# A quad's first difference behind the split before it, and buffers of their own for odd units' residual rows

## The chip, the cores and the metric

The program runs on one core of one Trainium2 chip. The metric is device time in microseconds (us) of one execution. The engines: PE (TensorE) multiplies matrices, DVE (VectorE) and ACT (ScalarE) do elementwise work, POOL (GpSimd) and SP (SyncE) here mostly issue transfers (DMAs). Each engine works its own queue of instructions in order.

## The reference

Two layers over 256 rows of 2048 values in float32, each with a norm, a wide input projection, attention over 32 heads of 128, a gate, and an output projection that is added to the residual:

```python
def reference(x, a_norm, a_w_in, a_rel_bias, a_w_out, kv_norm, kv_w, f_w, f_b,
              b_norm, b_w_in, b_w_out, final_norm):
    for layer in range(DEPTH):
        if layer < N_A_LAYERS:
            h = rms_norm(x, a_norm[layer])
            q, k, v, g = jnp.split(h @ a_w_in[layer], 4, axis=-1)
            o = chunked_relbias_attention(split_heads(q), split_heads(k), split_heads(v),
                                          a_rel_bias[layer]).reshape(b, s, D_INNER)
            x = x + (o * jax.nn.silu(g)) @ a_w_out[layer]
        else:
            ...
            h = rms_norm(x, b_norm[lb])
            q, g = jnp.split(h @ b_w_in[lb], 2, axis=-1)
            o = forgetting_attention(split_heads(q), k_sh, v_sh, cum_logf_h).reshape(b, s, D_INNER)
            x = x + (o * jax.nn.silu(g)) @ b_w_out[lb]
    return rms_norm(x, final_norm)
```

Keys, values and forget gates of layer B (`k_sh`, `v_sh`, `cum_logf_h`) are products of a norm of the same rows. The change touches the two output projections, the addition of the residual behind them, and the start of layer B.

## The kernel before

Matrix products are made exact to float32 by splitting: each weight block is loaded raw (`ao_raw`, 512 KB), ACT rounds it to a high part (`ao_hi`, L247), DVE takes the rest (`ao_lo`, L248), and PE makes three products of high and low parts (L184). The same happens in layer B with a gain factor (`bqg_hi` L242, `bqg_lo` L243). `Feed` loads blocks on SP in one given order, six raw buffers deep, and splits them three blocks ahead of PE.

The output projection of layer A runs from about 700 to 877 us, that of layer B from 1586 to 1754. Each has four units (u = 0 to 3) of 512 output columns and 16 blocks each. Unit u's sums of 256 rows stand in two PSUM tiles, `ao_acc` or `bo_acc`.

Part of the blocks are multiplied for two units at once, by a scheme that saves products (class `Quad`): the same block of two units, `one` and `two` (loaded one after the other, `two` later), is turned into four operands by differences on DVE. The first, A (L287), is `two − one`; the second, B (L288), takes one half of `two` from the other; later ones (L296, L297) write into `one`. Each operand is split (`quad_hi` L293 on ACT, `quad_lo` L294 on DVE). In layer A the pair of units 0 and 1 has three quads and the pair 2 and 3 has five, in layer B the pair 2 and 3 has five. Between two quads stand three plain blocks. The quads' partial products `p` are joined when the pair's last quad is done (L336 to L340, into `ao_quad`, read as `quads.comb`), and have to be added to each unit's rows.

Closing a unit (`ao_closed`): DVE adds the joined quads to the residual rows `xin` (L751, 128x1024) and then the two PSUM tiles (L753). `xin` was loaded by SP when the unit had four blocks left (L743, 512 KB, from `in_x`; in layer B from `x1d`). All `xin` share one buffer (tag "R"), so a load waits until the unit before has let go of it. SP stores the new rows to `x1d`. Then the rows are turned for layer B: for units 0 to 2 by a DVE transpose into `xinY` (L486) and 16 small POOL transfers into `xinZ` (L489, 32 KB each), which ACT and DVE split into `x1Th` and `x1Tl` (L150, L151). `xinY` is one buffer, so the next unit's transpose waits until all 16 transfers of the unit before have landed. Unit 3 is turned by PE (`xT`, L169), inside the first unit of layer B, `bqg0`, behind its second block (`{1: 99}` in the drive at L877). `bqg0` reads the turned rows in order, units 0 and 1 in its first four blocks, unit 2 from its fifth, unit 3 from its seventh.

At the end, `bo_closed` adds quads and sums likewise (L924, L889), squares the rows on ACT for the final norm (L890), and `finish_tile` scales and stores them.

The order of instructions on each engine is not that of the code: a scheduler places each instruction where its operands are expected, so an instruction that takes part in a dependency may be placed elsewhere. `feed.behind(dst, n)` (L261 to L264) is used for that: a tiny ACT copy of two columns of a block's high part into `dst`. Whatever then writes `dst` on another engine must follow that split.

Of the kernel before, what the change touches and what calls it, by code (L numbers as in the profile page):

```python
# [9 lines left out]
F32 = mybir.dt.float32  # L10
# [6 lines left out]
P = 128  # L17
S = 256
NT = S // P
# [16 lines left out]
UN = 512  # L36
# [23 lines left out]
B1_STEPS = {3: 1, 5: 1, 6: 2}  # L60
B2_STEPS = {1: 1}
OLD_B_STEPS = {0: 1, 1: 99}
# [3 lines left out]
def r32(ap):  # L66
    return ap.bitcast(F32)
# [8 lines left out]
def trunk(ctx, tc, x, x_t, gains, a_w_in, a_rel, a_w_out, kv_w, f_w, f_b, b_w_in, b_w_out, final_norm, out):  # L76
    nc = tc.nc
    pe, act, dve, pool, sp = nc.tensor, nc.scalar, nc.vector, nc.gpsimd, nc.sync
# [4 lines left out]
    att = ctx.enter_context(tc.tile_pool(name="att", bufs=1))  # L83
# [8 lines left out]
    def big_tile(shape, dt, name):  # L92
        return big.tile(shape, dt, name=name, tag="big")
# [46 lines left out]
    def advance(side, n=1):  # L140
        if side is not None:
            for _ in range(n):
                next(side, None)
# [18 lines left out]
    def x_to_T(src, k0):  # L162

        banks = []
        for c in range(0, 4, 2):
            ps = bank(f"xT_{k0 + c}")
            for i in range(2):
                for t in range(NT):
                    pe.transpose(ps[:, i * S + t * P:i * S + (t + 1) * P],  # L169
                                 src[t][:, (c + i) * P:(c + i + 1) * P], ident)  # L170
            banks.append(ps)
        for c in range(4):
            split_x1(banks[c // 2][:, c % 2 * S:(c % 2 + 1) * S], k0 + c)
            yield
# [102 lines left out]
    class Quad:  # L277
# [4 lines left out]
        def split(self, i):  # L282

            one, two = self.raw
            t = self.all.t[:, 0]
            if not i:
                dve.tensor_sub(t[:, :, 0], two[:, :, 0], one[:, :, 0])  # L287
                dve.tensor_sub(t[:, :, 1], two[:, :, 1], two[:, :, 0])  # L288
            src = [one, t, two[:, :, 1:], one][i]
            n = src.shape[2]  # L290
            hi = stream.tile([P, IL, KB, HN], F32R, name=f"quad_hi{i}", tag="hi", bufs=SPLIT)
            lo = stream.tile([P, IL, KB, HN], F32R, name=f"quad_lo{i}", tag="lo", bufs=SPLIT)
            act.activation(hi[:, :, :n], src, AF.Copy)  # L293
            dve.tensor_sub(lo[:, :, :n], src, r32(hi[:, :, :n]))  # L294
            if not i:
                dve.tensor_sub(one[:, :, 0], two[:, :, 1], t[:, :, 0])  # L296
                dve.tensor_sub(one[:, :, 1], one[:, :, 1], one[:, :, 0])  # L297
            return hi, lo
# [100 lines left out]
    ao_quads, bo_quads = Quads("ao", a_w_out), Quads("bo", b_w_out)  # L399
# [12 lines left out]
    feed = Feed(todo)  # L412
# [26 lines left out]
    def unit(lhs):  # L439
        yield from rest(Unit(lhs, next(order)))  # L440

    def rest(u):

        for b in range(u.nk // KB - u.left, u.nk // KB):
            u.step(b)
            yield u.acc
# [218 lines left out]
    def side_a(g, accs):  # L665
        tb = att.tile([P, HG, S], F32, name="tb", tag="tb")
        for lo_, hi_, c0 in ((0, CHUNK, CHUNK), (CHUNK, P, 0)):
            sp.dma_start(out=tb[lo_:hi_, :, c0:], in_=bass.AP(
                tensor=a_rel.tensor, offset=a_rel.offset + g * HG * NREL + REL + 1 - P + lo_ + c0,
                ap=[[1, hi_ - lo_], [NREL, HG], [1, S - c0]]))  # L670

        def biases():
            pool.memset(tb[:CHUNK, :, :CHUNK], NEG)
            return tb[:, :, ::-1], tb[:, :, P - 1::-1]

        qk = rows(UN, "qk")
        evac_scaled(accs["qk"], 0, UN, rsA, qk)
        yield

        def vg():  # L680
            return accs["v"], accs["g"]

        yield from attention(g, biases, qk, vg, halfA, oA, (pool, pool, pool, act), (2, 2), home)
# [5 lines left out]
    def drive(gen, side, steps, hooks={}, old=None, old_steps={}):  # L689

        acc = None
        for i, acc in enumerate(gen):
            advance(old, old_steps.get(i, 0))
            advance(side, steps.get(i, 0))
            if i in hooks:
                hooks[i]()
        return acc
# [12 lines left out]
    rs, prev = [], None  # L710
    for g in range(NG):
        accs = {}
# [7 lines left out]
        old, prev = prev, side_a(g, accs)  # L720
# [5 lines left out]
    x1T = Stat("x1T", KD)  # L726

    def x1_to_T(xin, u):
        z = turn(xin.rearrange("p t (c d) -> p (t c) d", d=P), NT * 4, "xin")
        xinT = z.rearrange("p i (t c) u -> p c t i u", t=NT)  # L730
        yield
        for i in range(4):
            feed.behind(x1T.h(u * 4 + i)[:, ::P][:, :, None], 2)
            for t in range(NT):
                split_x1(xinT[:, i, t], u * 4 + i,
                         lambda v: v[:, t * P:(t + 1) * P].rearrange("p (i u) -> p i u", u=SQ))
            yield

    xins, last = {}, []

    def load_xin(src, u):
        xins[u] = att.tile([P, NT, UN], F32, name="xin", tag="R")
        sp.dma_start(out=xins[u], in_=src[:, :, u * UN:(u + 1) * UN])  # L743

    def ao_begun(u, left):
        if left == 4:
            load_xin(xf, u)

    def ao_closed(u, acc):
        cs, xin = slice(u * UN, (u + 1) * UN), xins.pop(u)  # L750
        dve.tensor_add(xin, xin, ao_quads.comb[:, u % 2 * NT:u % 2 * NT + NT])  # L751
        for t in range(NT):
            dve.tensor_add(xin[:, t], acc[t], xin[:, t])  # L753
            sp.dma_start(out=x1d[:, t, cs], in_=xin[:, t])
        more = None
        if u < 3:
            more = x1_to_T(xin, u)
            next(more)
        else:
            last.append(x_to_T([xin[:, t] for t in range(NT)], u * 4))  # L760
        for t in range(NT):
            act.activation(att.tile([P, UN], F32, name="junk", tag="tb"), xin[:, t], AF.Square,
                           accum_out=ssq1[:, t, u:u + 1])
        return more and (more, [8, 1, 1, 1])
# [108 lines left out]
    old = prev = None  # L873
    fg = forget()
    for g in range(NG):
        accs = {}
        accs["qg"] = drive(unit(x1T), prev if g else last[0], B1_STEPS if g else {1: 99}, {}, old, OLD_B_STEPS)  # L877
        accs["kv"] = drive(unit(x1T), prev if g else fg, B2_STEPS if g else FORGET_STEPS, {2: lambda: open_b(accs)})
        old, prev = prev, side_b(g, accs)
        advance(prev)  # L880
# [36 lines left out]
    def bo_begun(u, left):  # L917
        if left == (4 if u else 1):
            load_xin(x1d, u)

    def bo_closed(u, acc):
        xin = xins.pop(u)
        if u > 1:
            dve.tensor_add(xin, xin, bo_quads.comb[:, u % 2 * NT:u % 2 * NT + NT])  # L924
        for t in range(NT):
            residual(acc, xin, u, t)
            if u == 2 and t == 1:
                norm_head()
            if u == 3:
                finish_tile(t)  # L930
# [48 lines left out]
```

## Time and profile before

| what | us |
|---|---|
| time, median of 3 runs | 1765.71 (1765.02 to 1766.46) |
| the profiled execution | 1764.38 |
| its span, first to last instruction | 1762.7 |
| PE busy | 1741.2 |
| DVE busy | 1244.9 |
| ACT busy | 1108.3 |
| POOL busy | 516.8 |

A row of the timeline reads: start, duration, engine, line, operation, what it writes and reads, count; in brackets how long the engine stood idle before and what ended that. SPq, ACTq and POOLq are the issue of transfers. A piece of the chain reads: start, duration, what. A window's row gives each engine's busy time in the stretch, the granted PE clock (1.00 is full), the transfer engines' busy share, and GB/s.

Outside the stretches that the prediction shows, PE stands still only at the start and in the B layer's attention, near 1545 us.

### The profile page before, as it was taken

To read this page: it belongs to the slowest core of one execution; us is meant where nothing else is said; L and a number is where in the kernel's file an instruction comes from. 1 tells how busy PE (TensorE), PEld (TensorE's weight loads), DVE (VectorE), ACT (ScalarE), POOL (GpSimd) and SP (SyncE) were. 2 spreads that over 40 slices of the span, in tenths; PEclk is the share of its full clock that TensorE was granted. 3 is DMA by queue.
4 is the path that set the end of the run, shared out by engine and by line. 5 is a ranking of instruction groups with operands and counts; after the bars stand their busy time and mean duration, and the time that the engine had idled before them with its cause. 6 is when DMAs were issued, how large, how long until landed. Compare 5 with 4: busy or idle time off the path is not lost.

```text
span 1762.7 us, 25633 instructions
## 1 busy us (share of the span) xinstructions
PE 1741.2 (99%) x8348; PEld 1531.0 (87%) x8348; DVE 1244.9 (71%) x1818; ACT 1108.3 (63%) x2102; POOL 516.8 (29%) x1071
## 2 busy tenths in 40 slices
PE   9999999999999999999999999999999999999997
PEld 7888888888888888887888888888888888888886
DVE  7666666666666686688877777777777777876687
ACT  6555555555555566556557777777777777765454
POOL 2333333333333333112104333333333333333000
PEclk9999999999999999999999999999999999999999
DMA  8777776767777677576767777776777777777664
GB/s 297 243 223 222 224 224 224 224 224 227 226 225 225 223 224 224 195 256 213 243 212 230 228 227 226 228 225 223 226 225 225 227 228 226 226 230 233 205 215 144
DMA packets 143653, 396.35 MB, mean 225 GB/s; under 512 B 31104, under 2 KB 38560, under 8 KB 143392
## 3 DMA queue, kind: packets, MB, share of 16 engines
q1 hardware_dynamic: 107472, 354.25, 63.1%
q0 software_dynamic: 32256, 37.29, 6.5%
q10 hardware_dynamic: 3792, 3.17, 0.6%
q8 instruction: 66, 1.08, 0.3%
q14 instruction: 67, 0.55, 0.1%
HBM read 351.05 MB, written 4.23 MB: 202 GB/s over the span
## 4 chain that ended last, share of the span: by engine, by line
PE 93%; DVE 3%; DMA 2%; issue 1%; ACT 1%; POOL 0%; ACTq 0%; SPq 0%; DVEq 0%; POOLq 0%
PE aqk_acc L184 19%; PE bkv_acc L184 19%; PE avg_acc L184 19%; PE bqg_acc L184 18%; PE bo_acc L184 6%; PE ao_acc L184 5%; PE op L574 1%; PE s0p L540 1%; DVE quad_lo L294 0%; DMA xinZ<-xinY 0%; PE op L517 0%; PE s1p L517 0%; PE s1p L516 0%; PE s1p L518 0%; PE op L518 0%
## 5 line engine op out<-in xcount | busy, mean ns | idle before, releaser
L489 POOL DMA_DIRECT2D sgZ<-sgY x512 | 251.0, 497 | 194.3 <-DVE sgY L486 90.6
L489 POOL DMA_DIRECT2D turned<-turned x448 | 219.9, 498 | 259.6 <-PE avg_acc L184 95.3
L243 DVE SCALAR_TENSOR_TENSOR bqg_lo<-bqg_raw,gain,bqg_hi 128x512 fp32r<-128x512 f32 x256 | 183.2, 753 | 84.3 <-ACT bqg_hi L242 84.2
L242 ACT ACTIVATE bqg_hi<-bqg_raw,gain 128x512 fp32r<-128x512 f32 x256 | 170.4, 714 | 106.7 <-PE bqg_acc L184 51.3
L248 DVE TENSOR_TENSOR avg_lo<-avg_raw,avg_hi 128x1024 fp32r<-128x1024 f32 x127 | 153.4, 1219 | 109.2 <-ACT avg_hi L247 108.0
L248 DVE TENSOR_TENSOR aqk_lo<-aqk_raw,aqk_hi 128x1024 fp32r<-128x1024 f32 x125 | 152.5, 1220 | 86.7 <-ACT aqk_hi L247 85.3
L247 ACT ACTIVATE avg_hi<-avg_raw 128x1024 fp32r<-128x1024 f32 x127 | 132.4, 1055 | 121.0 <-PE aqk_acc L184 68.5
L243 DVE SCALAR_TENSOR_TENSOR bkv_lo<-bkv_raw,gain,bkv_hi 128x512 fp32r<-128x512 f32 x256 | 181.2, 749 | 38.5 <-ACT bkv_hi L242 35.8
L184 PE MATMUL aqk_acc<-aqk_hi,xTh 128*128 128x512 f32 x512 | 191.4, 384 | 1.2 <-ACT aqk_hi L247 1.2
L184 PE MATMUL bqg_acc<-bqg_hi,x1Th 128*128 128x512 f32 x512 | 191.6, 384 | 0.0
L184 PE MATMUL avg_acc<-avg_hi,xTh 128*128 128x512 f32 x512 | 190.3, 382 | 0.0
L184 PE MATMUL aqk_acc<-aqk_lo,xTh 128*128 128x512 f32 x512 | 189.6, 381 | 0.0
L184 PE MATMUL aqk_acc<-aqk_hi,xTl 128*128 128x512 f32 x512 | 189.6, 381 | 0.0
L184 PE MATMUL bkv_acc<-bkv_hi,x1Th 128*128 128x512 f32 x512 | 189.2, 380 | 0.0
L184 PE MATMUL bqg_acc<-bqg_lo,x1Th 128*128 128x512 f32 x512 | 189.0, 379 | 0.0
L184 PE MATMUL bqg_acc<-bqg_hi,x1Tl 128*128 128x512 f32 x512 | 189.0, 379 | 0.0
L184 PE MATMUL bkv_acc<-bkv_lo,x1Th 128*128 128x512 f32 x512 | 189.0, 379 | 0.0
L184 PE MATMUL avg_acc<-avg_lo,xTh 128*128 128x512 f32 x512 | 189.0, 379 | 0.0
L184 PE MATMUL bkv_acc<-bkv_hi,x1Tl 128*128 128x512 f32 x512 | 189.0, 379 | 0.0
L184 PE MATMUL avg_acc<-avg_hi,xTl 128*128 128x512 f32 x512 | 189.0, 379 | 0.0
L247 ACT ACTIVATE aqk_hi<-aqk_raw 128x1024 fp32r<-128x1024 f32 x125 | 131.6, 1053 | 91.1 <-PE aqk_acc L184 43.5
L242 ACT ACTIVATE bkv_hi<-bkv_raw,gain 128x512 fp32r<-128x512 f32 x256 | 168.7, 712 | 22.9 <-PE bqg_acc L184 16.7
(297 smaller groups left out, 3563.8 us busy)
## 6 DMA issues: line engine op xcount, KB each, us to landing
bqg_raw<-in_b_w_in SPq DMA_DIRECT2D x128, 512.0 KB, 4.3
bkv_raw<-in_kv_w SPq DMA_DIRECT2D x128, 512.0 KB, 4.0
avg_raw<-in_a_w_in SPq DMA_DIRECT2D x127, 512.0 KB, 4.3
aqk_raw<-in_a_w_in SPq DMA_DIRECT2D x125, 512.0 KB, 4.2
ao_raw<-in_a_w_out SPq DMA_DIRECT2D x64, 512.0 KB, 4.4
bo_raw<-in_b_w_out SPq DMA_DIRECT2D x64, 512.0 KB, 4.2
sgZ<-sgY POOLq DMA_DIRECT2D x512, 40.0 KB, 4.1
turned<-turned POOLq DMA_DIRECT2D x448, 32.0 KB, 3.7
```

The source lines that it names most:

```text
L184: pe.matmul(acc[t], x[:, t * P:(t + 1) * P], w, start=t not in begun, stop=last and i == 2)
L242: act.activation(hi[:, :, j], raw[:, :, j], AF.Copy, scale=gk)
L243: dve.scalar_tensor_tensor(lo[:, :, j], raw[:, :, j], gk, r32(hi[:, :, j]), op0=OP.mult, op1=OP.subtract)
L247: act.activation(hi[:, :, j], raw[:, :, j], AF.Copy)
L248: dve.tensor_sub(lo[:, :, j], raw[:, :, j], r32(hi[:, :, j]))
L489: queues[j].dma_start(out=r32(z)[j * SQ:(j + 1) * SQ, i], in_=y[i * SQ:(i + 1) * SQ, j])
L540: pe.matmul(s0p[:, i], q0[:, i], qkT[:, HG + i, 0], start=True, stop=True)
L574: pe.matmul(op[:, i, P:], v1[:, i * DH:(i + 1) * DH], pT[:, i, NT], start=False, stop=i == HG - 1)
```

## The change

There are four edits. In `Quad.split` a copy by `feed.behind` is put ahead of the first difference, which ties A to the split of the block that precedes the quad. Rows `xin` of odd units get a tile of their own. The addition of the joined quads moves out of the closing: for odd units it comes when two blocks of the unit are left (in `add_combined`, L747 in the changed kernel). And unit 3's turn by PE goes behind the third block of `bqg0`. Lines behind L287 are one higher in the changed kernel, those behind L744 seven or more.

```diff
@@ -284,6 +284,7 @@
             one, two = self.raw
             t = self.all.t[:, 0]
             if not i:
+                feed.behind(t[:, :, 0, :1], -1)
                 dve.tensor_sub(t[:, :, 0], two[:, :, 0], one[:, :, 0])
                 dve.tensor_sub(t[:, :, 1], two[:, :, 1], two[:, :, 0])
             src = [one, t, two[:, :, 1:], one][i]
@@ -739,16 +740,22 @@
     xins, last = {}, []
 
     def load_xin(src, u):
-        xins[u] = att.tile([P, NT, UN], F32, name="xin", tag="R")
+        xins[u] = big_tile([P, NT, UN], F32, f"xin{u}") if u % 2 else att.tile([P, NT, UN], F32, name="xin", tag="R")
         sp.dma_start(out=xins[u], in_=src[:, :, u * UN:(u + 1) * UN])
+
+    def add_combined(quads, u):
+        dve.tensor_add(xins[u], xins[u], quads.comb[:, u % 2 * NT:u % 2 * NT + NT])
 
     def ao_begun(u, left):
         if left == 4:
             load_xin(xf, u)
+        if left == 2 and u % 2:
+            add_combined(ao_quads, u)
 
     def ao_closed(u, acc):
+        if u % 2 == 0:
+            add_combined(ao_quads, u)
         cs, xin = slice(u * UN, (u + 1) * UN), xins.pop(u)
-        dve.tensor_add(xin, xin, ao_quads.comb[:, u % 2 * NT:u % 2 * NT + NT])
         for t in range(NT):
             dve.tensor_add(xin[:, t], acc[t], xin[:, t])
             sp.dma_start(out=x1d[:, t, cs], in_=xin[:, t])
@@ -874,7 +881,7 @@
     fg = forget()
     for g in range(NG):
         accs = {}
-        accs["qg"] = drive(unit(x1T), prev if g else last[0], B1_STEPS if g else {1: 99}, {}, old, OLD_B_STEPS)
+        accs["qg"] = drive(unit(x1T), prev if g else last[0], B1_STEPS if g else {2: 99}, {}, old, OLD_B_STEPS)
         accs["kv"] = drive(unit(x1T), prev if g else fg, B2_STEPS if g else FORGET_STEPS, {2: lambda: open_b(accs)})
         old, prev = prev, side_b(g, accs)
         advance(prev)
@@ -917,11 +924,13 @@
     def bo_begun(u, left):
         if left == (4 if u else 1):
             load_xin(x1d, u)
+        if left == 2 and u == 3:
+            add_combined(bo_quads, u)
 
     def bo_closed(u, acc):
+        if u == 2:
+            add_combined(bo_quads, u)
         xin = xins.pop(u)
-        if u > 1:
-            dve.tensor_add(xin, xin, bo_quads.comb[:, u % 2 * NT:u % 2 * NT + NT])
         for t in range(NT):
             residual(acc, xin, u, t)
             if u == 2 and t == 1:
```

How the order of instructions moves, at three places. Names carry the unit (`ao2`, `ao3`), the block and a number of the tile.

First, DVE at the second quad of the pair of units 2 and 3 (near 805 to 814 us). Before:

```order
L294 TENSOR_TENSOR quad_lo3_7645<-ao2_raw0_7428,quad_hi3_7644 128x1024
L287 TENSOR_TENSOR ao_quad_6864<-ao3_raw1_7552,ao2_raw1_7550 128x2x256
L248 TENSOR_TENSOR ao2_lo9_7657<-ao2_raw9_7466,ao2_hi9_7656 128x1024
L248 TENSOR_TENSOR ao2_lo10_7669<-ao2_raw10_7484,ao2_hi10_7668 128x1024
L248 TENSOR_TENSOR ao2_lo11_7678<-ao2_raw11_7502,ao2_hi11_7677 128x1024
L288 TENSOR_TENSOR ao_quad_6864<-ao3_raw1_7552 128x2x256
L294 TENSOR_TENSOR quad_lo0_7694<-ao2_raw1_7550,quad_hi0_7693 128x1024
```

After:

```order
L295 TENSOR_TENSOR quad_lo3_7649<-ao2_raw0_7431,quad_hi3_7648 128x1024
L289 TENSOR_TENSOR ao_quad_6864<-ao3_raw1_7555 128x2x256
L248 TENSOR_TENSOR ao2_lo9_7661<-ao2_raw9_7469,ao2_hi9_7660 128x1024
L248 TENSOR_TENSOR ao2_lo10_7673<-ao2_raw10_7488,ao2_hi10_7672 128x1024
L248 TENSOR_TENSOR ao2_lo11_7682<-ao2_raw11_7506,ao2_hi11_7681 128x1024
L288 TENSOR_TENSOR ao_quad_6864<-ao3_raw1_7555,ao2_raw1_7553 128x2x256
L295 TENSOR_TENSOR quad_lo0_7699<-ao2_raw1_7553,quad_hi0_7698 128x1024
```

A (L287 before, L288 after) goes behind the three plain splits `ao2_lo9` to `ao2_lo11`; B (L288 before, L289 after) goes ahead of them, to the row where A stood. Both read `ao3_raw1`, the later load.

Second, SP and DVE where unit 1 closes (near 788 to 800 us). SP before, from the last load ahead of unit 1's rows to the second quad's blocks:

```order
L206 DMA ao2_raw9_7466<-in_a_w_out 128x1024
L743 DMA xin_7444<-in_x 128x2x512
L206 DMA ao2_raw10_7484<-in_a_w_out 128x1024
L206 DMA ao2_raw11_7502<-in_a_w_out 128x1024
L754 DMA x1d_6776<-xin_7444 128x512 x2
L206 DMA ao2_raw1_7550<-in_a_w_out 128x1024
L743 DMA xin_7862<-in_x 128x2x512
```

After:

```order
L206 DMA ao2_raw9_7469<-in_a_w_out 128x1024
L744 DMA xin_7868<-in_x 128x2x512
L206 DMA ao2_raw10_7488<-in_a_w_out 128x1024
L206 DMA ao2_raw11_7506<-in_a_w_out 128x1024
L761 DMA x1d_6776<-xin1_7447 128x512 x2
L206 DMA ao2_raw1_7553<-in_a_w_out 128x1024
L744 DMA xin3_8184<-in_x 128x2x512
L206 DMA ao3_raw1_7555<-in_a_w_out 128x1024
```

Unit 1's rows (`xin_7444` before, `xin1_7447` after) are loaded 36 rows ahead of their old place, unit 2's rows (`xin_7862`, `xin_7868`) stand where unit 1's stood, and unit 3's (`xin3_8184`) where unit 2's stood. DVE there before:

```order
L287 TENSOR_TENSOR ao_quad_6864<-ao3_raw0_7430,ao2_raw0_7428 128x2x256
L288 TENSOR_TENSOR ao_quad_6864<-ao3_raw0_7430 128x2x256
L248 TENSOR_TENSOR ao2_lo7_7499<-ao2_raw7_7392,ao2_hi7_7498 128x1024
L751 TENSOR_TENSOR xin_7444<-xin_7444,ao_quad_6864 128x1024
L753 TENSOR_TENSOR xin_7444<-ao1_acc0_7090,xin_7444 128x512
L753 TENSOR_TENSOR xin_7444<-ao1_acc1_7091,xin_7444 128x512
L248 TENSOR_TENSOR ao2_lo8_7547<-ao2_raw8_7410,ao2_hi8_7546 128x1024
L486 STREAM_TRANSPOSE xinY_7521<-xin_7444 128x1024
```

After:

```order
L248 TENSOR_TENSOR ao2_lo5_7466<-ao2_raw5_7341,ao2_hi5_7465 128x1024
L747 TENSOR_TENSOR xin1_7447<-xin1_7447,ao_quad_6864 128x1024
L248 TENSOR_TENSOR ao2_lo6_7485<-ao2_raw6_7350,ao2_hi6_7484 128x1024
L289 TENSOR_TENSOR ao_quad_6864<-ao3_raw0_7433 128x2x256
L248 TENSOR_TENSOR ao2_lo7_7503<-ao2_raw7_7395,ao2_hi7_7502 128x1024
L760 TENSOR_TENSOR xin1_7447<-ao1_acc0_7091,xin1_7447 128x512
L760 TENSOR_TENSOR xin1_7447<-ao1_acc1_7092,xin1_7447 128x512
L248 TENSOR_TENSOR ao2_lo8_7550<-ao2_raw8_7413,ao2_hi8_7549 128x1024
L288 TENSOR_TENSOR ao_quad_6864<-ao3_raw0_7433,ao2_raw0_7431 128x2x256
L487 STREAM_TRANSPOSE xinY_7524<-xin1_7447 128x1024
```

The add of the joined quads to unit 1's rows (L751, L747) goes ahead of two plain splits, and the row behind it is no longer that of the closing.

Third, DVE at the start of layer B (near 872 to 886 us). Before:

```order
L486 STREAM_TRANSPOSE xinY_8117<-xin_7862 128x1024
L243 SCALAR_TENSOR_TENSOR bqg0_lo0_8197<-bqg0_raw0_8078,gain_83,bqg0_hi0_8196 128x2x256
L243 SCALAR_TENSOR_TENSOR bqg0_lo1_8217<-bqg0_raw1_8090,gain_83,bqg0_hi1_8216 128x2x256 x2
L243 SCALAR_TENSOR_TENSOR bqg0_lo2_8237<-bqg0_raw2_8099,gain_83,bqg0_hi2_8236 128x2x256 x2
L243 SCALAR_TENSOR_TENSOR bqg0_lo3_8314<-bqg0_raw3_8144,gain_83,bqg0_hi3_8313 128x2x256
L751 TENSOR_TENSOR xin_8176<-xin_8176,ao_quad_6864 128x1024
L243 SCALAR_TENSOR_TENSOR bqg0_lo3_8314<-bqg0_raw3_8144,gain_83,bqg0_hi3_8313 128x2x256
L753 TENSOR_TENSOR xin_8176<-ao3_acc0_7638,xin_8176 128x512
L753 TENSOR_TENSOR xin_8176<-ao3_acc1_7639,xin_8176 128x512
```

After:

```order
L487 STREAM_TRANSPOSE xinY_8125<-xin_7868 128x1024
L243 SCALAR_TENSOR_TENSOR bqg0_lo0_8205<-bqg0_raw0_8086,gain_83,bqg0_hi0_8204 128x2x256
L747 TENSOR_TENSOR xin3_8184<-xin3_8184,ao_quad_6864 128x1024
L243 SCALAR_TENSOR_TENSOR bqg0_lo1_8226<-bqg0_raw1_8098,gain_83,bqg0_hi1_8225 128x2x256 x2
L243 SCALAR_TENSOR_TENSOR bqg0_lo2_8246<-bqg0_raw2_8107,gain_83,bqg0_hi2_8245 128x2x256 x2
L760 TENSOR_TENSOR xin3_8184<-ao3_acc0_7642,xin3_8184 128x512
L760 TENSOR_TENSOR xin3_8184<-ao3_acc1_7643,xin3_8184 128x512
L243 SCALAR_TENSOR_TENSOR bqg0_lo3_8322<-bqg0_raw3_8152,gain_83,bqg0_hi3_8321 128x2x256 x2
```

The add to unit 3's rows (`xin_8176`, `xin3_8184`) goes ahead of five splits of `bqg0`, and the closing adds go ahead of both splits of its fourth block, `bqg0_lo3`. On PE the eight matmuls of `xT` go from behind `bqg0`'s second block to behind its third, with 12 matmuls of 128x512 between.

## The prediction

> **What bounds the kernel now.** I read the page first, then the list of waits of PE (the TensorE matmul queue), then the chain and the engines' rows around each place where PE stands still.
>
> ```profile
> PE 1741.2 (99%) x8348; PEld 1531.0 (87%) x8348; DVE 1244.9 (71%) x1818; ACT 1108.3 (63%) x2102; POOL 516.8 (29%) x1071
> ```
>
> PE's waits, with the sum, their count and the longest:
>
> ```profile
> PE xT L169 <- DVE xin L753: 2.9, 2, 2.7
> PE op L516 <- ACT wideh L508: 2.6, 2, 2.2
> PE ao_acc L184 <- DVE ao_lo L248: 2.2, 1, 2.2
> PE bo_acc L517 <- DVE quad_lo L294: 0.9, 1, 0.9
> PE ao_acc L517 <- DVE quad_lo L294: 0.3, 1, 0.3
> PE p L517 <- DVE quad_lo L294: 0.3, 1, 0.3
> ```
>
> PE works in 99% of the span. No instruction of PE is removed, so the change can win only where PE waits, or behind PE's last matmul. It touches the waits named xT (2.9 us), ao_acc and p (2.2 + 0.3 + 0.3) and bo_acc (0.9), and the tail. The wait named op lies in the B layer's attention, where nothing moves. So the stake is some ten microseconds of 1764.38 (the profiled execution; its span is 1762.7), about 1.3 below the median of 1765.71. I take the sum against 1764.38 and carry it to the median.
>
> **Place 1: the second pair's first quads, 786 to 816 us.** DVE's rows:
>
> ```profile
> 793.82 1.23 DVE L751 TENSOR_TENSOR xin<-xin,ao_quad 128x1024 f32<-128x1024 f32 x1 [1.05 <-DMA xin<-in_x]
> 799.28 1.25 DVE L486 STREAM_TRANSPOSE xinY<-xin 128x1024 f32<-128x1024 f32 x1 [1.71 <-DMA xinZ<-xinY]
> 809.31 0.69 DVE L287 TENSOR_TENSOR ao_quad<-ao_raw,ao_raw 128x512 f32<-128x512 f32 x1 [1.98 <-DMA ao_raw<-in_a_w_out]
> 809.92 3.49 DVE L248 TENSOR_TENSOR ao_lo<-ao_raw,ao_hi 128x1024 fp32r<-128x1024 f32 x3
> 813.32 0.69 DVE L288 TENSOR_TENSOR ao_quad<-ao_raw 128x512 f32<-128x512 f32 x1
> ```
>
> The first difference (L287) waits 1.98 us for a weight block, and three splits stand behind it, the first of which PE needs at 811.19. The change ties L287 behind those splits. But the order of the changed kernel puts the second difference into the place that it leaves, and that one reads the later loaded block alone, the very block that L287 waited for. So DVE stops at the same point for the same transfer, and one 0.69 us instruction stands ahead of the splits as before. The tie itself costs a copy on ACT (ScalarE) for each of 13 quads:
>
> ```profile
> L264 ACT ACTIVATE x1Th<-ao_hi x2: 206/208/209, 793.8 to 825.4; 128x2 fp32r<-128x2 f32 x2
> 795.87 0.64 ACT L762 ACTIVATE junk<-xin 128x512 f32<-128x512 f32 x1 [1.87 <-DVE xin L753]
> ```
>
> 13 x 0.21 = 2.7 us of ACT, each beside idle time like the 1.87 us of the second row; without that cover all 2.7 would count. The copy follows its split at once and the new A waits for it only three splits later. **Term 1: 0**, between −2.2 (the wait gone after all) and +2.7. In the bo quads the swap is the same, and PE's 0.9 us there stays.
>
> What does move at this place is SP (the queue of the large transfers) against POOL's 16 small ones, which turn unit 0:
>
> ```profile
> 788.67 0.38 SPq L743 DMA_DIRECT2D xin<-in_x  x1
> 795.87 0.93 SPq L754 DMA_DIRECT2D x1d<-xin  x2
> 797.60 0.33 SPq L206 DMA_DIRECT2D ao_raw<-in_a_w_out  x1
> 795.64 1.02 POOL L489 DMA_DIRECT2D xinZ<-xinY  x2 [0.50 <-DMA xinZ<-xinY]
> 790.10 5.26 DMA xinZ<-xinY
> 796.17 2.99 DMA xinZ<-xinY
> 786.00:798.00 12.00, 12.00 (x57) 10.51 (x57) 8.94 (x10) 5.64 (x10) 7.87 (x16) 1.00 0.98 331
> ```
>
> Unit 1's residual rows are now loaded some 90 us before, in a buffer of their own, and the add (L751) no longer waits 1.05 us and no longer stands between the splits and unit 1's closing: two adds of 0.69 us instead of 1.23 + 2 x 0.69 behind a wait. So unit 1 closes about 2.4 us earlier (1.05 of the wait, 1.23 of the add, less little), and its two stores of 256 KB and the next 512 KB weight load are issued near 793.4, 794.1 and 795.2 in place of 795.87, 796.5 and 797.60. Now they stand ahead of the last two small transfers (795.64, 796.17), on which DVE's turn of unit 1 waits at 799.28. How much does that delay them? The transfer engines are 0.98 busy. The small transfer issued just behind a large load (790.10) took 5.26 us, the one with none right ahead (796.17) 2.99: 2.3 us more. By volume, 768 KB (786,432 bytes) at the window's 331 GB/s is 2.4 us. The lower end is 0, if small ones pass large ones. I take 2.2, since both rows lie at that end. DVE's turn, then the quads' splits, the release of the next load and PE's splits follow in one chain, so it all reaches PE. **Term 2: +2.2** (0 to +2.4).
>
> The place of unit 1's load, 788.67, is taken by unit 2's load of the same size, so nothing is added there.
>
> [...]
>
> **Place 2: the start of the B layer, 872 to 893 us.** The chain and the rows that end it:
>
> ```profile
> 876.45 6.37 DMA xin<-in_x
> 882.94 1.23 DVE xin L751
> 884.75 1.30 DVE xin L753 x2
> 886.09 0.99 PE xT L169 x7
> 885.58 0.30 PE L169 MATMUL xT<-ident,xin 128*128 128x128 f32 x1 [2.72 <-DVE xin L753]
> 885.01 0.98 POOL L489 DMA_DIRECT2D xinZ<-xinY  x2 [2.88 <-DMA xinZ<-xinY]
> 890.09 1.71 ACT L150 ACTIVATE x1Th<-xinZ 128x128 fp32r<-128x128 f32 x8 [3.15 <-DMA xinZ<-xinY]
> 892.09 0.38 PE L184 MATMUL bqg_acc<-bqg_hi,x1Th 128*128 128x512 f32 x1
> ```
>
> Unit 3's rows are loaded at 876.45 and land 6.37 us later; the add, the closing adds and PE's turn (xT) follow, and PE waits 2.9 us. After: the load goes out near 800.6 (when unit 1's buffer is free), the add stands before the last splits, and the turn comes after the third block of bqg0 in place of the second, 12 matmuls later. The closing adds then wait for PE's sums alone, long done. The wait goes, and with it what the pipeline loses at two stops (a matmul lasts 0.38 us at a step of 0.22, 0.16 each). **Term 3: −2.9 − 0.3 = −3.2** (−3.2 to −2.5).
>
> What is late next? The fifth block of bqg0 is the first to read unit 2's turned rows (x1Th<-xinZ). PE came to it near 892.0, 1.9 us after ACT began them at 890.09. Without the wait PE is there 3.2 us earlier, near 888.8. The small transfers land earlier too, since 512 KB go out of their way: POOL's last two (885.01) waited 2.88 us for a place, and 512 KB at the window's rate are 1.6 us. ACT then begins near 888.5, and the first rows' high and low parts take 0.5 us more: PE waits 0.2, or 2.0 if nothing comes earlier. I take 0.8, near the lower end. **Term 4: +0.8** (0 to +2.0).
>
> **Place 3: the tail.**
>
> ```profile
> 1743.76 4.01 DMA xin<-x1d
> 1747.79 1.23 DVE L924 TENSOR_TENSOR xin<-xin,bo_quad 128x1024 f32<-128x1024 f32 x1 [3.82 <-DMA xin<-x1d]
> 1753.22 0.38 PE L184 MATMUL bo_acc<-bo_hi,oBl 128*128 128x512 f32 x1
> 1753.71 0.69 DVE L889 TENSOR_TENSOR xin<-bo_acc,xin 128x512 f32<-128x512 f32 x1
> 1754.66 0.63 ACT L890 ACTIVATE junk<-xin 128x512 f32<-128x512 f32 x1 [0.41 <-DVE xin L889]
> ```
>
> The chain of waits runs through unit 3's load, and this looks like a gain of 3.82 us. It isn't: PE's last matmul is at 1753.22 whatever DVE does, and DVE's add behind it starts at 1753.71 and ends at 1754.40. ACT then begins 0.26 us late, held by the first half's work, which was late through the load. Only that goes. **Term 5: −0.25** (−0.5 to 0).
>
> **The sum.** 0 + 2.2 − 3.2 + 0.8 − 0.25 = −0.45: 1764.38 becomes 1763.9, and the median 1765.71 becomes **1765.3**: no change that a measurement of this kernel can tell, for which I take 0.2% (3.5 us: below 1762.2 or above 1769.2).
>
> **The rivals.**
>
> (a) *Small transfers aren't delayed.* Term 2 is 0: −2.65, 1763.1. For it: no row shows two queues' packets one by one, and a store of 256 KB that leaves the chip may not hold a turn within it. Against: the 5.26 us row.
>
> (b) *The split's wait goes.* If the second difference doesn't stand where I read it, or its block has landed by then, the 2.24 us before the split goes, and the half rate behind it:
>
> ```profile
> 811.19 0.48 PE L184 MATMUL ao_acc<-ao_lo,oAh 128*128 128x512 f32 x1 [2.24 <-DVE ao_lo L248]
> 812.39 0.64 PE L184 MATMUL ao_acc<-ao_hi,oAh 128*128 128x512 f32 x1
> 812.00:816.00 4.00, 4.00 (x12) 3.21 (x11) 3.83 (x5) 0.76 (x1) 1.98 (x5) 0.57 0.84 286
> ```
>
> From 812.4 some 8 matmuls go at a clock of about a half (0.57 in the window): 8 x 0.21 = 1.7 us. So −2.65 − 2.2 − 1.7 = −6.6: 1759.1. Against it: the order, and the load's issue, which hangs on the quad's own splits.
>
> (c) *A second stretch at half rate, the slower side.* If the chain of place 1 comes 2.2 us later, PE's wait of 0.3 us near 804.8 (p, L517) becomes 2.5, as long as the one that was followed by the half rate. If that decides, 1.7 us are added: −0.45 + 1.7 = +1.25, 1767.0; with term 4 at 2.0 and term 2 at 2.4, 1768.4. Against: the wait of 2.72 us at 885.58 was followed by no such stretch.
>
> [...]
>
> (d) *The change doesn't do what it says*: the transposes still wait, for a load that is held behind unit 1's buffer until late. Then terms 3 to 5 are 0 and only +2.2 stays: 1767.9. Against: the order has that load 30 rows ahead of its old place.
>
> **How the numbers follow.** Forecast 0.44, (a) 0.24, (b) 0.12, (c) 0.16, (d) 0.04. Faster by over 0.2%: all of (b) and the low end of (a), 0.15. Slower: the high end of (c) and (d), 0.06. Same: 0.79. The range runs from 1761.5, which is (a) with no stall at term 4 and 0.5 at the tail (1762.0) and 0.5 for the spread of the runs shown (0.7 below their median), to 1768.4, the high end of (c); it leaves out (b) and little else.
>
> **What would show it.** Step 1: the second difference waits near 809 to 812 for a weight block, and PE behind it about 2 us. Step 2: DVE's turn of unit 1 starts near 801.5, relative to the block before. Step 3: no wait named xT; step 4: a wait of bqg_acc on x1Th or x1Tl at bqg0's fifth block. Step 5: DVE's add of unit 3 directly behind that of unit 2, without a wait, and ACT's last square right behind DVE's add. Wrong I'd be if PE doesn't stop near 811, or if the turn of unit 1 comes no later.

## The result, and the profile after

| | us |
|---|---|
| before, 10 runs | 1766.28 (1763.92 to 1767.86) |
| changed, 10 runs | 1760.67 (1759.30 to 1763.77) |
| ratio | 0.9973, 95% interval 0.9963 to 0.9983 |
| ratio in two later comparisons | 0.9978 (0.9969 to 0.9986), 0.9973 (0.9962 to 0.9984) |

The ratios compare means of runs: the means of the first comparison differ by 4.8 us, its medians by 5.6. Over the three comparisons the changed kernel is faster by some 0.25%, about 4.4 us. The forecast was 1765.3 and no change that can be told; the range ended at 1761.5, 0.8 above the median that came. Yet the changed kernel's first profile looks as the prediction drew it. Its own execution took 1763.77 us, the longest of the ten, 0.6 below that of the first profile of before.

PE's waits in the changed kernel, between 780 and 900 us (sum, count, longest):

```profile
PE p L518 <- DVE quad_lo L295: 2.9, 2, 1.7
PE ao_acc L184 <- DVE ao_lo L248: 2.2, 1, 2.2
PE ao_acc L518 <- DVE quad_lo L295: 0.3, 1, 0.3
```

The wait for `ao_lo` stands at 2.2 as before, `p` has risen from 0.3 to 2.9, and `xT` (2.9) has gone. DVE's rows behind the first two, from its timeline:

```profile
795.39 0.68 DVE L288 TENSOR_TENSOR ao_quad<-ao_raw,ao_raw 128x512 f32<-128x512 f32 x1
802.61 1.25 DVE L487 STREAM_TRANSPOSE xinY<-xin 128x1024 f32<-128x1024 f32 x1 [6.54 <-DMA xinZ<-xinY]
...
812.56 0.69 DVE L289 TENSOR_TENSOR ao_quad<-ao_raw 128x512 f32<-128x512 f32 x1 [1.91 <-DMA ao_raw<-in_a_w_out]
813.17 3.49 DVE L248 TENSOR_TENSOR ao_lo<-ao_raw,ao_hi 128x1024 fp32r<-128x1024 f32 x3
```

The second difference (L289) waits 1.91 us for the block that L287 waited 1.98 us for, and the three splits follow it. The turn of unit 1 stands idle 6.54 us for unit 0's small transfers, where it was 1.71; part of that is only that DVE comes to it sooner, and the turn itself starts 3.3 us later than before (802.61 against 799.28). SP's issues and the chain of waits there:

```profile
793.67 0.92 SPq L761 DMA_DIRECT2D x1d<-xin  x2
795.50 0.33 SPq L206 DMA_DIRECT2D ao_raw<-in_a_w_out  x1
```

```profile
791.02 7.17 DMA xinZ<-xinY
798.20 0.28 issue
798.47 4.01 DMA xinZ<-xinY
```

The stores and the load now go out ahead of the last small transfer, which takes 4.01 us where it took 2.99. In this execution the piece before it, issued at 791.02 and so ahead of the stores, was slow too (7.17 against 5.26); the rows don't show how much of that is the stores', which were issued while it was under way. The start of layer B, one window of PE (busy time and count in the first columns), before and after:

```profile
870.00:900.00 30.00, 27.07 (x129) 23.41 (x128) 21.66 (x41) 19.11 (x45) 8.85 (x18) 1.00 0.75 228
```

```profile
870.00:900.00 30.00, 30.00 (x145) 26.33 (x144) 24.98 (x44) 20.07 (x46) 8.83 (x18) 1.00 0.78 249
```

PE doesn't stop there any more, at the fifth block neither. And the tail, DVE and ACT:

```profile
1739.73 2.35 DVE L747 TENSOR_TENSOR xin<-xin,bo_quad 128x1024 f32<-128x1024 f32 x2
1753.42 0.69 DVE L896 TENSOR_TENSOR xin<-bo_acc,xin 128x512 f32<-128x512 f32 x1 [4.28 <-PE bo_acc L184]
```

```profile
1754.14 0.63 ACT L897 ACTIVATE junk<-xin 128x512 f32<-128x512 f32 x1 [4.55 <-DVE xin L896]
```

Both adds stand together without a wait, DVE has 4.28 us to spare before PE's last sums, and ACT's square starts when DVE's add ends (1753.42 + 0.69 = 1754.11).

So the two profiled executions differ by about what was forecast (0.6 us, forecast 0.45), and the times of all runs by several microseconds more. That was the question for the experiments.

### The profile page after: what moved, and what is told of

Same layout as the page of the kernel before. It is cut to its first block, busy times and chain, and to the rows that moved or that the text cites. A ratio compares the mean times of both kernels' runs of the same rounds, so it can differ in the third digit from the quotient of the medians.

```text
span 1762.0 us, 25649 instructions
## 1 busy us (share of the span) xinstructions
PE 1741.4 (99%) x8348; PEld 1527.5 (87%) x8348; DVE 1244.3 (71%) x1818; ACT 1109.4 (63%) x2115; POOL 519.5 (29%) x1071
## 4 chain that ended last, share of the span: by engine, by line
PE 92%; DMA 3%; DVE 2%; ACT 1%; issue 1%; POOL 1%; SPq 0%; DVEq 0%; POOLq 0%; ACTq 0%
PE bkv_acc L184 19%; PE bqg_acc L184 19%; PE aqk_acc L184 18%; PE avg_acc L184 18%; PE bo_acc L184 7%; PE ao_acc L184 4%; DMA sgZ<-sgY 1%; PE op L575 1%; PE s0p L541 1%; DMA xinZ<-xinY 1%; DVE quad_lo L295 1%; PE p L519 0%; PE p L518 0%; PE p L517 0%; PE op L518 0%
## 5 line engine op out<-in xcount | busy, mean ns | idle before, releaser
L247 ACT ACTIVATE aqk_hi<-aqk_raw 128x1024 fp32r<-128x1024 f32 x125 | 131.6, 1052 | 91.1 <-PE aqk_acc L184 43.5
L242 ACT ACTIVATE bkv_hi<-bkv_raw,gain 128x512 fp32r<-128x512 f32 x256 | 168.8, 712 | 25.5 <-PE bqg_acc L184 18.9
```

Of the source, the lines that this page charges most:

```text
L242: act.activation(hi[:, :, j], raw[:, :, j], AF.Copy, scale=gk)
L247: act.activation(hi[:, :, j], raw[:, :, j], AF.Copy)
```

## The experiments

Each kernel's trace was cut at PE's matmuls: from the first of the output projection of layer A to the first of layer B (**ao**), from there to the first of `bkv` (**bqg0**), from the first of `bo` to the last matmul (**bo**), and from there to the end (**tail**). "Slow" counts matmuls of 128x512 at a step of 0.41 to 0.43 us instead of 0.22, all the way from ao to bo. The stretch between bqg0 and bo isn't shown; its mean differs by 0.3 us between three profiles of before and three of changed.

| kernel | ao | bqg0 | bo | tail | slow | time (runs) | ratio to before |
|---|---|---|---|---|---|---|---|
| before, 1st profile | 167.2 | 24.9 | 167.0 | 9.4 | 8 | | |
| before_b | 167.9 | 26.4 | 166.6 | 9.4 | 9 | 1763.55 (1) | |
| before_c | 167.7 | 26.3 | 166.7 | 9.3 | 12 | 1764.08 (1) | |
| changed, 1st profile | 170.4 | 21.6 | 166.8 | 9.0 | 7 | 1760.67 (10) | 0.9973 |
| after_again | 169.1 | 21.6 | 166.9 | 9.1 | 8 | 1761.50 (12) | 0.9978 (0.9969 to 0.9986) |
| after_c | 170.0 | 21.6 | 166.5 | 9.1 | 6 | 1760.30 (7) | 0.9973 (0.9962 to 0.9984) |
| no_tie | 169.5 | 21.6 | 167.0 | 9.1 | 0 | 1761.60 (12) | 0.9982 (0.9973 to 0.9990) |
| both_tied | 170.5 | 21.6 | 167.7 | 9.1 | 8 | 1762.17 (11) | 0.9985 (0.9977 to 0.9994) |
| third_block | 167.2 | 23.4 | 166.5 | 9.4 | 0 | 1762.12 (11) | 0.9981 (0.9972 to 0.9989) |
| tie_only | 166.8 | 27.3 | 166.7 | 9.5 | 2 | 1763.56 (12) | 0.9993 (0.9982 to 1.0005) |
| u3_own | 166.5 | 21.6 | 166.8 | 9.1 | 0 | 1758.50 (8) | 0.9967 (0.9956 to 0.9978) |
| u3_no_tie | 167.9 | 21.6 | 166.7 | 9.2 | 8 | 1758.33 (7) | 0.9969 (0.9956 to 0.9982) |
| after_turn | 171.7 | 21.6 | 167.1 | 9.0 | 7 | 1762.79 (12) | 0.9986 (0.9977 to 0.9995) |
| u3_turn | 169.7 | 21.6 | 167.0 | 9.1 | 6 | 1761.85 (11) | 0.9982 (0.9972 to 0.9992) |

Times of different rows stem from up to four chips; the ratio is to the kernel before on the same chip, and only ratios are compared.

**after_again and after_c: the changed kernel, two more profiles.**

> The changed kernel again, for a second profile and more times. The first profile (1763.77 us) was the longest of ten executions (median 1760.67). Theory M: the gain is PE's wait for the last unit's rows at the start of layer B (2.9 us before, none after) and 0.25 at the tail; the wait of 2.2 us for ao_lo stays in every execution. What differs between executions is how long the turn of unit 1 (xinY) waits for the small transfers: 6.5 us in the first profile, PE 2.9 us on p; in an execution near 1760.6 it should be about 3 us less, PE under 0.8 us on p. Rival R: in most executions the wait for ao_lo is gone too (with its eight slow matmuls, 3.9 us in all), and the first profile was the exception: then ao_lo doesn't stand in PE's waits.

> The changed kernel, a third profile, beside three of before. Stage times so far (PE, first matmul to first matmul): ao 170.4 and 169.1 (before 167.2, 167.9, 167.7), bqg0 21.6 and 21.6 (before 24.9, 26.4, 26.3, the last two with a stretch of slow matmuls behind the wait for xT). Theory M2: the gain is 3.3 us in every execution at bqg0, and 1.5 more in those where the kernel before falls to the half rate there, less about 2 in ao: bqg0 21.6 again, ao 168.8 to 170.5. Rival: ao varies by executions as much as it differs between kernels, so it may come out at 167.

`ao_lo` stands in PE's waits with 2.1 and 2.2 us, so rival R falls. The turn of unit 1 stands idle 5.76 and 6.55 us. ao is 1.2 to 3.2 longer than in the profiles of before: the loss isn't an accident of one execution, and the expectation that it would shrink in a faster one was wrong (PE's wait for `p` is 2.1 and 2.9, expected under 0.8). Measured from the first matmul of ao, the turn of unit 1 starts after 91.1 to 92.2 us in the three profiles of changed and after 89.0 to 89.4 in those of before.

**before_b and before_c: the kernel before, two more profiles.**

> The kernel before, unchanged, for a second profile: does its first profile (1764.38 us, below the median of 1765.45 in 35 executions) stand for the others? Stage times of PE to compare, from the first matmul of a stage to the first of the next: ao 167.2, first unit of layer B (bqg0) 24.9, rest as far as bo 658.9 with a wait of 2.2 near 1545, bo 167.0, tail 9.4. Theory M: bqg0 stays at 24.5 to 25.5 and ao at 166.5 to 169, the wait near 1545 differs between executions by up to 2.6 us, as it does between the changed kernels (0 to 2.2). Rival S: that wait stands in every execution of the kernel before and is what the change shortens.

> As before_b, a third profile of the kernel before: theory M expects bqg0 at 24.5 to 25.5, ao at 166.5 to 169; rival S a wait of about 2.2 us near 1545 again.

bqg0 takes 26.4 and 26.3, not 24.5 to 25.5. PE's rows in before_b behind the wait for `xT`, and the clock of that stretch:

```profile
886.39 0.30 PE L169 MATMUL xT<-ident,xin 128*128 128x128 f32 x1 [2.54 <-DVE xin L753]
886.90 1.71 PE L169 MATMUL xT<-ident,xin 128*128 128x128 f32 x7 [0.21 <-DVE xin L753]
888.26 0.77 PE L184 MATMUL bqg_acc<-bqg_hi,x1Th 128*128 128x512 f32 x1
888.83 0.63 PE L184 MATMUL bqg_acc<-bqg_lo,x1Th 128*128 128x512 f32 x1
889.26 0.63 PE L184 MATMUL bqg_acc<-bqg_hi,x1Tl 128*128 128x512 f32 x1
889.69 0.63 PE L184 MATMUL bqg_acc<-bqg_hi,x1Th 128*128 128x512 f32 x1
```

```profile
886.00:892.00 6.00, 5.40 (x21) 4.64 (x22) 2.98 (x9) 2.60 (x10) 0.63 (x2) 0.72 0.98 240
```

The clock is granted at 0.72 of full on average there; the seven transposes take 1.71 us instead of 0.99, and the matmuls behind go at a step of 0.43. The wait itself is no longer than in the first profile (2.54 against 2.72). Of the four profiles with this wait (tie_only is the fourth, with 0.75 in the same window), three have the slow stretch and the first didn't. It costs 1.4 to 1.5 us (26.4 and 26.3 against 24.9). What the traces show of the execution that escapes it stands in the last section. The wait near 1545 us differs between executions in both kernels, as theory M expected: 2.2, none and 0.3 before, 1.7, 1.4 and none after.

**no_tie: the changed kernel without the tie.**

```diff
-                feed.behind(t[:, :, 0, :1], -1)
```

> The changed kernel without the tie: the first difference stands ahead of the splits again. Theory M: the tie is worth nothing, since the second difference waits at the same place for the same block: within 1 us of the changed kernel, some 5 us below before, wait for ao_lo 2.2 us in the profile. Rival R (the tie takes the wait away in most executions): about 3.9 us above the changed kernel, so 1.5 to 2 us below before.

0.9982 against 0.9978 in the same comparison, with intervals that overlap almost wholly: the tie is worth nothing that these runs can tell. PE's waits are about as with it:

```profile
PE p L517 <- DVE quad_lo L294: 2.9, 2, 1.7
PE ao_acc L184 <- DVE ao_lo L248: 2.6, 2, 2.4
```

**tie_only: the tie alone, in the kernel before.**

```diff
             if not i:
+                feed.behind(t[:, :, 0, :1], -1)
                 dve.tensor_sub(t[:, :, 0], two[:, :, 0], one[:, :, 0])
```

> The kernel before with the tie alone. Here the scheduler puts the second difference behind one plain split of DVE (in the changed kernel it stands ahead of all three). Theory M2: the 2.2 us for ao_lo go, as in u3_own, but a wait of the same size comes 11 us later at the quad's own splits, so the time is within 1.5 us of before, bqg0 24.9 to 26.4. Rival R (the tie is a gain of its own): 2 to 4 us below before, ao 164 to 165.5.

0.9993, no gain. Here the second difference stands behind one plain split, and PE's waits of that stretch read:

```profile
PE xT L169 <- DVE xin L754: 3.8, 2, 3.6
PE p L518 <- DVE quad_lo L295: 1.2, 1, 1.2
PE ao_acc L518 <- DVE quad_lo L295: 1.1, 2, 0.8
PE ao_acc L517 <- ACT quad_hi L294: 1.0, 1, 1.0
PE ao_acc L184 <- DVE ao_lo L248: 0.2, 1, 0.2
```

The wait for `ao_lo` is down to 0.2, but 1.0 on `quad_hi` and 0.8 more on `quad_lo` have come, at the operands of the next quad, 11 us later.

**both_tied: what the edit's name seems to promise.**

```diff
-                feed.behind(t[:, :, 0, :1], -1)
+                for j in range(KB):
+                    feed.behind(t[:, :, j, :1], -1)
```

> Both differences tied, so that three plain splits of DVE stand ahead of both at the second quad of the second pair. Theory M: this is what takes the wait away: PE no longer waits 2.2 us for ao_lo near 811 us, and the slow matmuls behind it (8 x 0.21 = 1.7 us) go or shrink: 2 to 4 us below the changed kernel, near 1757. Rival R: the tie of the first difference already does it: no difference to the changed kernel. A third way: the wait only moves on to the quad's own splits (quad_lo), for the same block: within 1 us.

The third way came. PE doesn't wait for `ao_lo` at all, and then:

```profile
824.09 0.48 PE L518 MATMUL ao_acc<-quad_hi,oAh 128*128 128x512 f32 x1 [1.87 <-ACT quad_hi L295]
825.35 0.63 PE L519 MATMUL ao_acc<-quad_lo,oAh 128*128 128x512 f32 x1 [0.78 <-DVE quad_lo L296]
825.77 0.63 PE L520 MATMUL ao_acc<-quad_hi,oAl 128*128 128x512 f32 x1
```

1.87 and 0.78 us, and the slow matmuls behind, at the second quad's own operands. ACT, which splits them, had stood idle just before, in front of a split of unit 1's turned rows that waits for small transfers:

```profile
822.58 0.51 ACT L150 ACTIVATE x1Th<-xinZ 128x128 fp32r<-128x128 f32 x2 [5.29 <-DMA xinZ<-xinY]
823.00 1.04 ACT L295 ACTIVATE quad_hi<-ao_raw 128x1024 fp32r<-128x1024 f32 x1
```

With tie_only this makes two kernels in which the wait moved on to the next quad instead of going.

**third_block: the place of unit 3's turn alone.**

```diff
-...last[0], B1_STEPS if g else {1: 99}, {}, old, OLD_B_STEPS)
+...last[0], B1_STEPS if g else {2: 99}, {}, old, OLD_B_STEPS)
```

> The kernel before with one edit alone: unit 3's turn by PE behind the third block of bqg0. Theory M: PE comes to the turn 2.6 us later (12 matmuls), at 885.5, and the rows are ready at 886.0: of 3.2 us about 2.5 go, less up to 2.0 that the fifth block may wait for unit 2's rows: 1.5 to 2.5 us below before. Rival B (the early load and the buffer are what is needed): no gain, under 0.7 us, since the load lands when it did and the wait moves to the fifth or seventh block.

0.9981: most of the change's gain with one number, and without its loss in ao (167.2). That is 3.4 us below before, more than the 1.5 to 2.5 expected. The granted clock on record for each run shows where the rest may come from: 0.9981 on average in these 11 runs against 0.9970 in the 35 of before, which is 2.0 us of the span. PE still waits 0.4 for `xT` and 0.5 at a later split, bqg0 is 23.4 against 24.9 to 27.3, and there is no slow stretch in it.

**u3_own and u3_no_tie: unit 1 in the shared buffer again.**

```diff
-...f"xin{u}") if u % 2 else att.tile([P, NT, UN], F32, name="xin", tag="R")
+...f"xin{u}") if u == 3 else att.tile([P, NT, UN], F32, name="xin", tag="R")
```

> The changed kernel, but only unit 3 has a buffer of its own; unit 1 shares one as in the kernel before, so it closes as late as there and its stores and the next weight load are issued behind unit 0's last small transfers again. Theory M: the 2 to 3 us that the changed kernel loses in the ao stage (167.2 before, 170.4 and 169.1 after) come back: ao 166.5 to 167.7, bqg0 21.6 and the tail 9.05 as in the changed kernel: about 2 us below the changed kernel, near 1759. Rival: the ao stage stays at 169 to 170.5, then the tie or the early add costs it, not the stores.

> As u3_own, and without the tie. In u3_own the scheduler puts the second difference behind one plain split, here both differences stand as in the kernel before. Theory M: the split that PE waits for near 811 us comes up to 0.7 + 2.0 us later than in u3_own; if the wait counts, this is 1 to 2.7 us above u3_own; if the wait only moves on to the quad's own split, within 1 us. ao stage 167.2 +- 0.5, or 165.5 when no matmuls run slow.

Both are at 0.9967 and 0.9969, with ao at 166.5 and 167.9. u3_no_tie and no_tie differ in unit 1's buffer alone, and so in when its rows are loaded and when it closes; the chain of waits in each, first no_tie, then u3_no_tie:

```profile
791.09 6.04 DMA xinZ<-xinY
797.13 0.28 issue
797.40 5.12 DMA xinZ<-xinY
...
802.65 1.25 DVE xinY L486
```

```profile
790.15 6.04 DMA xinZ<-xinY
796.19 0.28 issue
796.47 0.49 POOL xinZ L489
796.96 2.78 DMA xinZ<-xinY
...
799.86 1.25 DVE xinY L486
```

Up to there the chains are alike (6.04 us each); then the last small transfer takes 5.12 against 2.78 us, 2.3 more, and ao is 169.5 without slow matmuls against 167.9 with eight of them. The kernels before and after part in the same way: the last small transfer takes 4.01, 4.33 and 4.87 us in the three profiles of the changed kernel, where by SP's rows of the first two the next load was issued ahead of it (at 795.50 and 794.47, the transfer at 798.47 and 796.35), and 2.99 in the first profile of before, where the load comes behind it (797.60 against 796.17). So unit 1's own buffer is what costs the changed kernel in ao, and by these rows its early closing, which puts stores and load ahead of that transfer, is how. u3_own has no slow matmuls and no wait for `ao_lo` in its profile, yet the two agree in time, so that difference of 1.3 us in ao is one of executions or is lost elsewhere. By their ratios these are the best versions tried, some 1 to 2 us ahead of the changed kernel; the intervals overlap. The tie makes no difference between the two either.

**after_turn and u3_turn: a second `xinY` buffer.**

```diff
-        z = turn(xin.rearrange("p t (c d) -> p (t c) d", d=P), NT * 4, "xin")
+        home = u == 1 and [big_tile([P, NQ, NT * 4, SQ], F32, "xinY1"),
+                           att.tile([P, NQ, NT * 4, SQ], F32, name="xinZ", tag="Z")]
+        z = turn(xin.rearrange("p t (c d) -> p (t c) d", d=P), NT * 4, "xin", home=home)
```

> The changed kernel with a second xinY buffer: unit 1's turn on DVE no longer waits until unit 0's 16 small transfers have landed. If that wait is what costs the changed kernel its 2 to 3 us in ao, ao falls to 166.5 to 168 (part of the wait goes on to the next row that needs those transfers, x1Tl, one row later), bqg0 stays at 21.6: 1.5 to 3 us below the changed kernel. Rival (the loss in ao comes from the late load of the quad's second block alone): ao stays at 169 to 170.

> u3_own with the second xinY buffer: both ways of easing the chain together. Theory M2: unit 1's turn stands ahead of the landing, 1.2 us of DVE's chain are done while it waits: ao 165.3 to 166.5 against 166.5 in u3_own, time 0 to 1.2 us below it, near 1758. Rival: nothing more to win there, since the first quad's own loads set the pace: equal within 0.5 us in ao.

Neither came as expected: ao is 171.7 and 169.7, longer than without the buffer. DVE and SP of after_turn at the third quad:

```profile
821.01 1.23 DVE L295 TENSOR_TENSOR quad_lo<-ao_raw,quad_hi 128x1024 fp32r<-128x1024 f32 x1 [0.65 <-ACT quad_hi L294]
825.03 0.69 DVE L289 TENSOR_TENSOR ao_quad<-ao_raw 128x512 f32<-128x512 f32 x1 [2.80 <-DMA ao_raw<-in_a_w_out]
825.64 3.49 DVE L248 TENSOR_TENSOR ao_lo<-ao_raw,ao_hi 128x1024 fp32r<-128x1024 f32 x3
```

```profile
819.56 0.38 SPq L746 DMA_DIRECT2D xin<-in_x  x1
820.05 9.43 SPq L206 DMA_DIRECT2D ao_raw<-in_a_w_out  x5
```

The new tile takes a place in the big pool, unit 3's rows are therefore loaded at 819.56, 16 us later than in the changed kernel, and just ahead of the third quad's later block, for which DVE then waits 2.80 us. PE's wait for `ao_lo` rises to 4.9 in two. Up to the second quad the buffer did what it was meant to: measured from the first matmul of ao, DVE took up that quad's later block after 99.6 us, against 101.0 to 102.2 in three profiles of the changed kernel. It was paid for with those waits one quad later; what it would bring without that isn't shown.

## Why the prediction was right or wrong

**The tie (term 1, 0): right.** The second difference stood where it was read, waited 1.91 us for the same block, and no_tie, tie_only and the pair of u3_own and u3_no_tie put the tie's worth at nothing that can be told. Rival (b) expected 3.9 us from a split that goes ahead; both_tied shows that even with the wait for `ao_lo` gone entirely, it comes back 13 us later.

**The small transfers behind the stores (term 2, +2.2): right in what comes late, and in size on average.** ao is 169.8 on average of three profiles against 167.6 of three before: +2.2. The agreement to the tenth is luck, since single profiles of one kernel differ by up to 1.2; in the changed kernel's first profile it was +3.2, above the bound of 2.4. The price of one small transfer behind a load, 2.3 us by two rows, came out at 2.3 between no_tie and u3_no_tie. Rival (a), by which small transfers aren't delayed, doesn't hold: the last one takes 4.01, 4.33 and 4.87 us in the three profiles of changed against 2.99 in the first of before.

**The wait for unit 3's rows (term 3, −3.2): right in what goes, and mis-sized.** The wait went in every profile, but with it went a stretch at a reduced clock that the profile of before didn't show: 25.9 on average of three profiles against 21.6, −4.3. This is the step that failed. The prediction knew what such a stretch costs (1.7 us at place 1, in rival (c)), and it dismissed one here because "the wait of 2.72 us at 885.58 was followed by no such stretch". That was one execution, and the exception of four. The same wait comes with it (2.54 us in before_b) and without it (2.72 in the first profile); the last section has what the traces show of that. The granted clock on record for every run gives the size over all of them: 0.9970 on average in 80 runs of before and 0.9980 in 29 of the changed kernel, 1.8 us of the span, where the sum had nothing. Those figures don't say where in a run the clock was lost; third_block, which moves only the turn of unit 3, has nearly all of it (2.0).

**The fifth block (term 4, +0.8): wrong, 0.** bqg0 takes 21.6 with no wait in any kernel that has both edits. In the first profiles ACT began unit 2's rows at 890.24, about as before (890.09), though the stage began 3.3 us later: sooner by that much against the stage, and not by the 1.6 us of one 512 KB load. Part of that is the execution: the profiles of before have it 9.8 to 12.6 us after the stage's first matmul, those of changed 9.4 to 9.6. The term also set PE's coming 3.2 us earlier against the old time of those rows, and left out that term 2 has PE come later.

**The tail (term 5, −0.25): right**, 9.39 to 9.06 on average of three, −0.33; and right that the 3.82 us of waiting there were nearly all slack, since PE's last matmul sets the end.

**Rivals (c) and (d)** didn't come: the chain's longer waits were followed by 6 to 8 slow matmuls as before, and by none in no_tie.

**The sum.** By three profiles each it is +2.2 − 4.3 − 0.33 = −2.4, and the profiled executions' own times differ by as much (1764.0 on average before, 1761.5 after). That the two first profiles differ by 0.6, so close to the 0.45 of the forecast, is luck: there term 2 was 1.0 too low and term 4 was 0.8 too high. The times of all runs differ by 4.4, and the forecast of no change that can be told did not hold: by the ratio the median of 1765.71 becomes 1760.9, 0.6 below the range.

Of the 2 us between −2.4 and −4.4, about 1.4 is which executions were profiled: those of before took 0.4 to 1.6 us less than the means of their comparisons, and those of the changed kernel 2.6 more, 0.5 less and 0.9 less. The clock is part of it on the side of the changed kernel: its three traces have 0.9977 on average and its runs 0.9980, while those of before agree (0.9970 both). The rest isn't settled. The hint was there ahead: the profile of before lay 1.3 us below the median, and carrying the sum over to the median took that difference for a constant.

## What to carry to other kernels

Before costing a wait of two or three microseconds on TensorE, ask what the clock does behind it, in several executions: here the slow stretch added some 1.4 us to a price of 3.3 in two of three profiles of before, and nothing in the one that was read. Here a wait of 2.54 us was followed by the stretch and one of 2.72 was not, so the price of such a wait is an average. Work that becomes free earlier issues its transfers earlier; look for what small transfers they overtake (here the last one took 4.01 us in place of 2.99), and who waits for those. And moving one instruction of a tight stretch moved the wait twice here; what gained was to let PE do other work first (the third block instead of the second), which is one number in the code.

## What the runs showed of the hardware that was not expected

A reduced clock isn't tied to the length of the wait ahead of it alone: in no_tie PE waited 2.9 us for `p` in two stops, 0.6 for the quads in two and 2.6 for `ao_lo` in two, the longest 2.4, and no slow matmul followed (the clock is 1.00 from 812 to 820), while 2.54 us in before_b were followed by the stretch at 0.72. The clock records of the two first profiles have one reduced stretch each between the kernel's first microseconds and PE's last matmul: 3.41 us at 0.50, from 812.34 before and from 815.37 in the changed kernel. Each begins a whole number of 3.4133 us after the first step to the full clock: 802.13 = 235 x 3.4133 before, 805.54 = 236 x 3.4133 in the changed kernel. With both spans cut into pieces of that length from that step on, PE stands idle 2.2 us in the piece ahead of the reduced one in either kernel; the most in any other piece is 1.8 us before and 1.5 in the changed kernel, and the piece behind those is at 1.00. The piece that before_b's wait lies in, idle for 2.75 us, and the one behind it (the first figures are the time and PE's busy time, the clock is the third from the end):

```profile
883.58:886.99 3.41, 0.66 (x4) 0.23 (x3) 3.23 (x5) 0.71 (x2) 0.98 (x2) 1.00 0.73 208
886.99:890.40 3.41, 3.41 (x12) 3.03 (x13) 1.17 (x2) 0.73 (x3) 0.00 (x0) 0.50 0.89 295
```

In the first profile of before the border at 884.02 parts the wait: PE stands idle 1.2 us in the piece ahead of it and 1.8 in the one behind, and the clock stays at 1.00:

```profile
880.61:884.02 3.41, 2.25 (x11) 1.63 (x9) 1.08 (x1) 0.60 (x1) 1.29 (x3) 1.00 0.95 336
884.02:887.43 3.41, 1.64 (x11) 1.43 (x12) 3.33 (x6) 1.45 (x4) 0.98 (x2) 1.00 0.59 152
887.43:890.84 3.41, 3.41 (x18) 2.99 (x17) 0.41 (x2) 0.75 (x4) 0.00 (x0) 1.00 1.08 297
```

The first step to the full clock comes 10.21 us into the span before and 9.82 in the changed kernel. By this reading the same wait can come with the stretch or without it, by where it falls in these pieces. That is read from three traces; no run was made to try it, and what sets the granted clock isn't shown.

The last small transfer (32 KB) of unit 0's turn, issued by POOL at 798.47, took 4.01 us in the changed kernel's first profile, where SP had issued two stores of 256 KB (793.67) and a load of 512 KB (795.50) ahead of it. In the first profile of before, issued at 796.17 with the load behind it (797.60), it took 2.99. It took 4.33 and 4.87 in the two later profiles of the changed kernel, 5.12 in no_tie and 2.78 in u3_no_tie. So here the small transfer took longer with the large ones ahead, though they are on another queue; how the transfer engines share their time isn't shown.
